# Modulation products moved from GpSimd and ScalarE to VectorE, and spread over three feed-forward stretches

## The chip, the cores and the metric

The kernel runs on one core of one Trainium2 chip. The core has TensorE (PE in the profile's rows, PEld for its weight loads), VectorE (DVE), ScalarE (ACT), GpSimd (POOL) and SyncE (SP, which here only issues DMAs). Each engine takes its own instructions in order, and they wait for one another through semaphores. The metric is the device time of one execution in microseconds (us).

## The reference, cut to what matters

Two blocks run one after the other, each with two layers, on 512 tokens of width 1024. A layer of the first block is a mixer, an attention over a memory of 256 tokens, and a gated feed-forward network (FFN). A layer of the second block is a local attention and an FFN, for the 512 tokens and, in its first layer alone, for a context of 256 tokens too. The second block scales and shifts its normalised inputs, and gates its outputs, with a modulation that depends on two vectors only, `c` for the tokens and `c_ctx` for the context:

```python
for i in range(DEPTH):                    # the second block, DEPTH = 2
    last = i == DEPTH - 1
    mod = silu(c) @ w_mod[i] + b_mod[i]          # 1024 -> 6 * 1024
    mod_c = silu(c_ctx) @ w_mod[i] + b_mod[i]
    sh1, sc1, gt1, sh2, sc2, gt2 = jnp.split(mod[:, None, :], 6, axis=-1)
    sh1c, sc1c, gt1c, sh2c, sc2c, gt2c = jnp.split(mod_c, 6, axis=-1)
    h = modulate(rmsnorm(x, g_attn[i]), sh1, sc1)
    hc = modulate(rmsnorm(ctx, g_attn[i]), sh1c, sc1c)
    ...                                   # attention; x = x + gt1 * (o @ w_out)
    h = modulate(rmsnorm(x, g_ffn[i]), sh2, sc2)
    x = x + gt2 * conv_ffn(h, ...)
    if not last:
        ...                               # the same for ctx with gt1c, sh2c, sc2c, gt2c
```

So `w_mod` (two layers of 24 MB) meets only two vectors, and in the last layer the context needs nothing beyond `sh1c` and `sc1c`, the first 16 of 48 groups of 128 outputs.

## The kernel before

All activations lie with their features on the 128 partitions, in tiles of 128 x 512 (tokens) or 128 x 256 (context). A linear layer is exact to nearly full precision by splitting: each operand is the sum of a rounded high part and a low part, and `lin` issues three matmuls for each 128 x 128 weight tile (high x high, high x low, low x high). A weight of 128 x 1024 (eight of those tiles) comes in through `wload` (L318 to L332): SyncE loads it into a buffer `wr` (two of them), ScalarE writes its high part `wh` (L314), VectorE its low part `wl` (L331, `wr - wh`); there are three buffers of `wh` and three of `wl`. TensorE needs both parts of a weight, and gives them back when it is through with it. A new activation is split in the same way (`split`: L314 on ScalarE, then L317 on VectorE).

`ffn1` is the first block's FFN, 22 units of 2816 / 128 features. For each unit `up` makes two products of 24 matmuls, scales each with the norm's factor out of PSUM (L1178), and runs a three-tap convolution over the tokens (one tap on ScalarE, L1181, two on VectorE, L1183), a Silu, the gate product (L1186) and the split. The units come in parts of 6, 6, 5 and 5 (`F1_PARTS`); each part's down-projection (8 tiles of features, `down`, added to `x` at L1199) waits in a queue and is issued tile by tile among the units of the next part.

`ffn2` is the second block's FFN. In the first layer it runs two streams, tokens and context, with the same weights: `up` copies PSUM out on ScalarE, `conv` does all three taps on VectorE (L2025, L2027), `gate` the gate and split. It has parts of 8, 7 and 7 units (`FF_PARTS`), and each part's down-projection follows its units at once (`down`, L2084). Matmul results go to PSUM banks with the tags L, S, PT and O; the up-products of this stretch use L (two banks; S for some of the first eight).

The modulation doesn't use TensorE. `mod_steps` (L1246) is a generator. A step loads one 128 x 512 tile of `w_mod` (256 KB, 96 of them for a layer), multiplies it with the two vectors, which lie broadcast over the partitions, and sums each product along its row into one column of `mparts`. Of eight products VectorE does two, in one instruction with a row sum (L1282); GpSimd does six as a plain product (L1284), which ScalarE copies with a row sum three products later (L1262). `mem_attn` of first-block layer `i` starts the steps of second-block layer `i`, and `ffn1` goes on with them after each unit: two steps for a unit of the first part, five for the others (`F1_MOD`). So each of the two first-block FFNs carries a whole layer of the modulation, 192 products.

[...]

Of the kernel before, what the change touches and what calls it, by code (L numbers as in the profile page):

```python
# [14 lines left out]
AF = mybir.ActivationFunctionType  # L15
# [22 lines left out]
MSTEP = (0,1,4,1,2)  # L38
MDN = (0,0,2)
MH = 48  # L40
MLAG = 3
# [21 lines left out]
MPF = 4  # L63
MODV = (0,4)
# [23 lines left out]
F1_MOD = (2, 5, 5, 5)  # L88
# [170 lines left out]
class Builder:  # L259
# [804 lines left out]
    def mem_attn(self, i, f, mh, K, fn):  # L1064
# [17 lines left out]
        self.steps = self.mod_steps(i, 0, 96)  # L1082
# [66 lines left out]

    def step(self, n, r):  # L1150
# [6 lines left out]
    def ffn1(self, i, f, fn):  # L1157
# [5 lines left out]

        def bank():
            self.bank += 1
            return self.p(FTAGS[self.bank % len(FTAGS)])

# [78 lines left out]
    def mod_steps(self, i, n0, n1):  # L1246
        nc = self.nc
        cv = []
        for v in range(2):
            for e in range(2):  # L1250
# [4 lines left out]
            yield  # L1255
        part = self.mparts
        late = []

        def add(k):
            while len(late) > k:  # L1260
                o, t = late.pop(0)
                nc.scalar.activation(t, t, AF.Copy, accum_out=o)  # L1262

        ws = {}

        def load(n):
            if n < n1:
                ws[n] = self.t("A", [P, 512])
                nc.sync.dma_start(out=ws[n], in_=self.a["w_mod"][i, n // 2, n % 2])

        for n in range(n0, n0 + MPF):
            load(n)
        for n in range(n0, n1):
            load(n + MPF)
            m, e = divmod(n, 2)
            w = ws.pop(n)
            for v in range(2):
                t = self.t("A", [P, 512])
                self.modn += 1
                o = part[:, v, e, m:m + 1]  # L1280
# [6 lines left out]
            yield  # L1287
        add(0)
        if n1 == 96:
            for v in range(2):  # L1290
                mo = self.mod[i][:, :, v]
                nc.vector.tensor_add(out=mo, in0=part[:, v, 0], in1=part[:, v, 1])
# [931 lines left out]
```

## Time and profile before

| | before |
|---|---|
| median of 3 runs (lowest to highest), us | 3841.25 (3839.11 to 3844.32) |
| the profiled execution: its time, us | 3832.78 |
| its span, first to last instruction, us | 3831.0 |
| busy: TensorE matmuls / weight loads | 3675.2 (96%) / 3062.5 (80%) |
| busy: VectorE / ScalarE / GpSimd | 2669.1 (70%) / 1842.9 (48%) / 1001.0 (26%) |
| mean granted TensorE clock | 0.988 of full speed |

The span holds these stretches: the first block's mixers and memory attentions with its FFNs at about 694 to 1090 us and 1740 to 2142 us, the second block's first attention, its first FFN (both streams) at about 2617 to 3172 us, the second attention, and the last FFN (tokens alone) from 3464 us to the end. A share of busy time is a mean over stretches with different limits, and TensorE's busy time is longer where its clock is lower.

### The profile page before, as it was taken

The numbers are of one execution on the slowest core, as the hardware profiler recorded it, in microseconds if no ns is written. First come the engines' busy times: TensorE is split into PE (matmuls) and PEld (weight loads), VectorE is DVE, ScalarE is ACT, GpSimd is POOL, SyncE is SP. The second block draws the span as 40 slices with busy tenths as digits, with TensorE's granted clock in tenths as the row PEclk, the third lists the DMA queues.
The fourth block names the chain that finished last, engine by engine and source line by source line (L and its number), as shares of the span: only waits on it lengthen the run. The fifth ranks groups of instructions, "written<-read, shape, count | busy, mean of one in ns | idle before, by whom it ended". The sixth has DMA issues, their size and how long they took to land. (4 is left out here: it accounts for less than half of the span.)

```text
span 3831.0 us, 55553 instructions
## 1 busy us (share of the span) xinstructions
PE 3675.2 (96%) x21300; PEld 3062.5 (80%) x21300; DVE 2669.1 (70%) x4599; ACT 1842.9 (48%) x3532; POOL 1001.0 (26%) x688
## 2 busy tenths in 40 slices
PE   8999999999899999999999899899999999999999
PEld 6777788777778777887777899778888888888887
DVE  7768756889977687668998753777545547657555
ACT  5645634455555456344555454774222225554232
POOL 1223243467621121234666212321000012100000
PEclk9999999999999999999999999999999999999999
DMA  3222143344422211333444332322212212012232
GB/s 112 67 72 67 51 127 100 111 154 157 146 91 72 72 57 56 126 105 102 165 155 150 123 104 92 108 73 72 66 61 61 66 56 74 15 40 93 94 95 93
DMA packets 128714, 354.39 MB, mean 93 GB/s; under 512 B 14144, under 2 KB 26816, under 8 KB 128448
## 3 DMA queue, kind: packets, MB, share of 16 engines
q1 hardware_dynamic: 127440, 349.62, 28.6%
q8 instruction: 168, 2.75, 0.3%
q10 hardware_dynamic: 1008, 1.21, 0.1%
q14 instruction: 98, 0.80, 0.1%
HBM read 346.58 MB, written 4.19 MB: 92 GB/s over the span
## 5 line engine op out<-in xcount | busy, mean ns | idle before, releaser
L304 PE MATMUL L<-A,wh 128*128 128x512 f32 (+1 forms) x6408 | 1861.5, 375 | 19.5 <-ACT wh L314 8.8
L304 PEld LDWEIGHTS L<-A,wh 128*128 128x128 f32 x6408 | 1148.0, 189 | 241.7 <-ACT wh L314 13.1
L304 PE MATMUL L<-A,wl 128*128 128x512 f32 (+1 forms) x3204 | 1194.9, 373 | 20.4 <-DVE wl L331 19.8
L314 ACT ACTIVATE wh<-wr 128x1024 fp32r<-128x1024 f32 (+4 forms) x562 | 561.9, 1001 | 787.7 <-PE L L304 429.8
L331 DVE TENSOR_TENSOR wl<-wr,wh 128x1024 fp32r<-128x1024 f32 (+4 forms) x503 | 658.7, 1311 | 327.2 <-ACT wh L314 319.1
L304 PEld LDWEIGHTS L<-A,wl 128*128 128x128 f32 x3204 | 604.7, 189 | 137.5 <-DVE wl L331 26.3
L1284 POOL TENSOR_TENSOR A<-A,A 128x512 f32<-128x512 f32 x288 | 482.3, 1706 | 280.6 <-DMA A<-in_w_mod 169.2
L304 PE MATMUL S<-A,wh 128*128 128x512 f32 (+1 forms) x944 | 301.0, 400 | 25.6 <-ACT wh L314 14.7
L331 POOL TENSOR_TENSOR wl<-wr,wh 128x1024 fp32r<-128x1024 f32 (+1 forms) x59 | 139.4, 2363 | 547.4 <-ACT wh L314 473.4
L304 PE MATMUL L<-wh,A 128*128 128x256 f32 x1440 | 272.7, 285 | 2.3 <-ACT A L1309 2.0
L304 PE MATMUL PT<-A,wh 128*128 128x512 f32 (+1 forms) x904 | 262.1, 375 | 0.0
L304 PEld LDWEIGHTS S<-A,wh 128*128 128x128 f32 x944 | 180.9, 195 | 70.8 <-ACT wh L314 16.5
L1183 DVE SCALAR_TENSOR_TENSOR A<-A,vec,A 128x512 f32<-128x512 f32 x176 | 215.2, 1223 | 30.6 <-ACT A L1181 26.4
L304 PEld LDWEIGHTS L<-wh,A 128*128 128x128 f32 x1440 | 226.0, 189 | 8.1 <-issue 4.2
L304 PE MATMUL O<-A,A 128*64 128x128 f32 (+3 forms) x2528 | 228.1, 288 | 4.2 <-DVE A L648 3.6
L433 POOL TENSOR_TENSOR acc<-acc,A 128x512 f32<-128x512 f32 (+1 forms) x44 | 53.8, 1222 | 672.1 <-ACT A L427 670.2
L304 PE MATMUL L<-wl,A 128*128 128x256 f32 x720 | 204.6, 284 | 4.6 <-DVE wl L331 4.6
L304 PEld LDWEIGHTS O<-A,A 128*64 128x64 f32 (+1 forms) x2528 | 168.5, 143 | 48.6 <-issue 24.0
L304 PE MATMUL S<-A,wl 128*128 128x512 f32 (+1 forms) x472 | 189.8, 402 | 17.8 <-DVE wl L331 17.6
L1262 ACT ACTIVATE A<-A 128x512 f32<-128x512 f32 x288 | 177.3, 618 | 38.5 <-POOL A L1284 38.3
L304 PEld LDWEIGHTS PT<-A,wh 128*128 128x128 f32 x904 | 166.7, 191 | 32.7
L314 ACT ACTIVATE A<-A 128x512 fp32r<-128x512 f32 (+2 forms) x202 | 115.3, 571 | 147.4 <-DVE A L1186 78.1
(323 smaller groups left out, 5249.7 us busy)
## 6 DMA issues: line engine op xcount, KB each, us to landing
wr<-in_w_up SPq DMA_DIRECT2D x176, 512.0 KB
A<-in_w_mod SPq DMA_DIRECT2D x192, 256.0 KB
wr<-in_w_qkv SPq DMA_DIRECT2D x62, 512.0 KB
wr<-in_w_in SPq DMA_DIRECT2D x60, 512.0 KB
wr<-in_w_down SPq DMA_DIRECT2D x32, 448.0 KB
wr<-in_w_down SPq DMA_DIRECT2D x32, 384.0 KB
wr<-in_w_down SPq DMA_DIRECT2D x32, 320.0 KB
wr<-in_w_os SPq DMA_DIRECT2D x16, 512.0 KB
```

Source lines behind the costliest of these rows:

```text
L304: self.last_mm = self.nc.tensor.matmul(out, lhsT=l, rhs=r, start=start, stop=stop, skip_group_check=True)
L314: self.nc.scalar.activation(h, src, AF.Copy)
L331: eng.tensor_sub(out=l[:, :cols], in0=r[:, :cols], in1=h[:, :cols].bitcast(F32))
L433: self.mark_p = (add or nc.gpsimd).tensor_add(out=acc.t, in0=acc.t, in1=dst)
L1183: ve.scalar_tensor_tensor(out=ac, in0=u[:, tap:tap + S], scalar=cw(tap), in1=ac, op0=ALU.mult, op1=ALU.add)
L1262: nc.scalar.activation(t, t, AF.Copy, accum_out=o)
L1284: nc.gpsimd.tensor_mul(out=t, in0=w, in1=cv[2 * v + e])
```

## The change

Every product of the modulation that is still made is made on VectorE, in one instruction with its row sum (now L1274). GpSimd's products and ScalarE's row sums are gone. The steps are laid out anew:

- Second-block layer 0: `mod_steps(0, 24 * i, 24 * i + 24)`. The memory attention and FFN of first-block layer 0 do output groups 0 to 23, those of layer 1 groups 24 to 47: 48 steps and 96 products each.
- Second-block layer 1: `mod_steps(1, 0, 48)` inside `ffn2` of the second block's first layer, its steps set off after the up-products (0.7 a product, none in a part's last unit) and the down-products (1.2 each). Context products are made for 16 of the 48 groups: 96 steps, 128 products.
- A pass of `mod_steps` goes first through the half `e = 0` of all its groups and then through `e = 1`. It loads two vectors for each half, and two tiles of `w_mod` ahead (`MPF`, four before).
- That FFN has parts of 6, 6, 5 and 5 units, and all its results rotate through PSUM tags L, S and PT.

```diff
-MSTEP = (0,1,4,1,2)
+MSTEP = (0,0.5)
...
-MPF = 4
-MODV = (0,4)
+MPF = 2
...
-F1_MOD = (2, 5, 5, 5)
+F1_MOD = (1, 2.5, 2.5, 2.5)
+F2_PARTS = ((0, 6), (6, 6), (12, 5), (17, 5))
+F2_MOD = (0.7, 1.2)
...
-        self.steps = self.mod_steps(i, 0, 96)
+        self.steps = self.mod_steps(0, 24 * i, 24 * i + 24)
...
-    def mod_steps(self, i, n0, n1):
+    def mod_steps(self, i, m0, m1):
...
+        nv = lambda m: 2 if i < DEPTH - 1 or m < 16 else 1
+        for e in range(2):
+            cv = []
+            for v in range(2):
                 c = self.t("A", [P, 512])
                 nc.sync.dma_start(out=c, in_=self.a["cvec"][v, e])
                 nc.scalar.activation(c, c, AF.Silu)
                 cv.append(c)
...
-                if self.modn % 8 in MODV:
-                    nc.vector.scalar_tensor_tensor(out=t, in0=w, scalar=1.0, in1=cv[2 * v + e], op0=ALU.mult, op1=ALU.mult, accum_out=o)
-                else:
-                    nc.gpsimd.tensor_mul(out=t, in0=w, in1=cv[2 * v + e])
-                    late.append((o, t))
-            add(MLAG)
-            yield
...
+            for m in range(m0, m0 + MPF):
+                load(m)
+            for m in range(m0, m1):
+                load(m + MPF)
+                w = ws.pop(m)
+                for v in range(nv(m)):
+                    t = self.t("A", [P, 512])
+                    nc.vector.scalar_tensor_tensor(out=t, in0=w, scalar=1.0, in1=cv[v], op0=ALU.mult, op1=ALU.mult,
+                                                   accum_out=part[:, v, e, m:m + 1])
+                yield
...
+        bank = self.next_bank if both else lambda: self.p("L")
+        fparts = F2_PARTS if both else FF_PARTS
+        if both:
+            self.bank = 0
+            self.steps = self.mod_steps(1, 0, 48)
...
+                        if both and j < j0 + nj - 1:
+                            self.step(4 * j + 2 * e + 1 - s, F2_MOD[0])
...
                 down(m, s)
+                if both:
+                    self.step(n, F2_MOD[1] if pi < 3 else 100)
```

The order of TensorE's matmuls in the first block's FFNs stays as it was. Three places show what moves.

GpSimd, in the first block's first FFN, before: nothing but the modulation's products stands in its queue (`A` tiles: the product, the tile of `w_mod`, a vector). Here are six of them.

```order
L1284 TENSOR_TENSOR A_7124<-A_6958,A_5899 128x512
L1284 TENSOR_TENSOR A_7126<-A_6958,A_5944 128x512
L1284 TENSOR_TENSOR A_7132<-A_6966,A_5902 128x512
L1284 TENSOR_TENSOR A_7139<-A_6973,A_5899 128x512
L1284 TENSOR_TENSOR A_7141<-A_6973,A_5944 128x512
L1284 TENSOR_TENSOR A_7147<-A_7115,A_5902 128x512
```

In the changed kernel this FFN has no row on GpSimd at all: all 288 rows of L1284 are gone, and the last sum of squares of the memory attention is followed by the next mixer's first rows.

VectorE, in the third part of the same FFN, before: the low parts of weights (`wl`), the scaling out of PSUM, the taps, the gate, a down tile added to `x`, the split of the unit, and then its share of the products.

```order
L331 TENSOR_TENSOR wl_8106<-wr_8104,wh_8105 128x768
L1177 MEMSET A_8027 128x2
L1183 SCALAR_TENSOR_TENSOR A_7992<-A_7989,vec,A_7992 128x512 x2
L1178 TENSOR_TENSOR A_8027<-PT_7996,rs_6308 128x512
L331 TENSOR_TENSOR wl_8132<-wr_8130,wh_8131 128x1024
L1183 SCALAR_TENSOR_TENSOR A_8030<-A_8027,vec,A_8030 128x512 x2
L1186 TENSOR_TENSOR A_8030<-A_7992,A_8030 128x512
L1199 TENSOR_TENSOR x<-x,L_8077 128x512
L331 TENSOR_TENSOR wl_8170<-wr_8168,wh_8169 128x1024
L317 TENSOR_TENSOR A_8037<-A_8030,A_8036 128x512
L1282 SCALAR_TENSOR_TENSOR A_8044,mparts<-A_7876,A_5947 128x512
L1282 SCALAR_TENSOR_TENSOR A_8059,mparts<-A_7891,A_5947 128x512
```

The changed kernel at such a unit:

```order
L331 TENSOR_TENSOR wl_7578<-wr_7576,wh_7577 128x1024
L1184 SCALAR_TENSOR_TENSOR A_7477<-A_7474,vec,A_7477 128x512 x2
L1179 TENSOR_TENSOR A_7512<-S_7481,rs_6280 128x512
L331 TENSOR_TENSOR wl_7616<-wr_7614,wh_7615 128x1024
L1184 SCALAR_TENSOR_TENSOR A_7515<-A_7512,vec,A_7515 128x512 x2
L1187 TENSOR_TENSOR A_7515<-A_7477,A_7515 128x512
L1200 TENSOR_TENSOR x<-x,PT_7549 128x512
L331 TENSOR_TENSOR wl_7672<-wr_7670,wh_7671 128x768
L317 TENSOR_TENSOR A_7522<-A_7515,A_7521 128x512
L1274 SCALAR_TENSOR_TENSOR A_7525,mparts<-A_7405,A_5938 128x512
L1274 SCALAR_TENSOR_TENSOR A_7527,mparts<-A_7405,A_5941 128x512
L1274 SCALAR_TENSOR_TENSOR A_7529,mparts<-A_7411,A_5938 128x512
```

The work of the unit is the same; four to six products stand behind its split where two or three stood.

VectorE, in the second block's first FFN, at the start of a part's down-projection, before (a part of eight units): after the unit's last split come, for each tile of features, two results added out of PSUM and the next weight's low part.

```order
L317 TENSOR_TENSOR A_25895<-A_25811,A_25894 128x512
L2020 MEMSET A_26393 128x1
L2021 MEMSET A_26393 128x1
L2084 SCALAR_TENSOR_TENSOR A_18673<-L_25898,mod_108,A_18673 128x256
L2084 SCALAR_TENSOR_TENSOR x<-L_25899,mod_108,x 128x512
L331 TENSOR_TENSOR wl_26075<-wr_26073,wh_26074 128x1024
L2084 SCALAR_TENSOR_TENSOR A_18673<-L_25956,mod_108,A_18673 128x256
L2084 SCALAR_TENSOR_TENSOR x<-L_25988,mod_108,x 128x512
L331 TENSOR_TENSOR wl_26133<-wr_26131,wh_26132 128x1024
```

The changed kernel at the end of its first part of six units: the last rows ahead of the low part of the fourth down weight (`S`, `PT`: PSUM results; L1274: products; L2082: results added). Between the part's last split and the first row here stand five more products and two more results.

```order
L1274 SCALAR_TENSOR_TENSOR A_24868,mparts<-A_24825,A_24138 128x512
L1274 SCALAR_TENSOR_TENSOR A_24892,mparts<-A_24832,A_24135 128x512
L1274 SCALAR_TENSOR_TENSOR A_24894,mparts<-A_24832,A_24138 128x512
L2082 SCALAR_TENSOR_TENSOR x<-S_24870,mod_108,x 128x512
L1274 SCALAR_TENSOR_TENSOR A_24924,mparts<-A_24864,A_24135 128x512
L1274 SCALAR_TENSOR_TENSOR A_24926,mparts<-A_24864,A_24138 128x512
L1274 SCALAR_TENSOR_TENSOR A_24930,mparts<-A_24890,A_24135 128x512
L2082 SCALAR_TENSOR_TENSOR A_17802<-PT_24896,mod_108,A_17802 128x256
L1274 SCALAR_TENSOR_TENSOR A_24932,mparts<-A_24890,A_24138 128x512
L1274 SCALAR_TENSOR_TENSOR A_24956,mparts<-A_24922,A_24135 128x512
L1274 SCALAR_TENSOR_TENSOR A_24958,mparts<-A_24922,A_24138 128x512
L331 TENSOR_TENSOR wl_24963<-wr_24961,wh_24962 128x768
```

So 14 products and four results, where two results stood before each weight, come between the last split and that weight's low part. For the two parts that follow, five products stand in that place.

## Rows read from the trace of the kernel before

**Rows 1.** Four FFN stretches: length, busy PE PEld DVE ACT POOL, PEclk, DMA.

```profile
694.00:1090.00 396.00, 375.12 (x1580) 298.75 (x1579) 354.32 (x435) 217.18 (x443) 242.48 (x144) 0.98 0.45 144
1740.00:2142.00 402.00, 376.11 (x1573) 300.19 (x1572) 351.22 (x455) 219.86 (x457) 226.39 (x135) 0.96 0.44 142
2617.00:3172.00 555.00, 552.22 (x3139) 480.86 (x3137) 308.47 (x668) 161.93 (x267) 15.01 (x12) 1.00 0.20 62
3464.00:3831.00 367.00, 362.44 (x1604) 294.42 (x1602) 218.06 (x368) 118.71 (x162) 0.00 (x0) 1.00 0.30 95
```

**Rows 2.** The chain that ended last, its final piece: start, length, what.

```profile
3464.96 361.49 PE L L304 x1597
```

**Rows 3.** TensorE's waits in 694:1090, 1740:2142: us in total, times, longest.

```profile
PE S L304 <- DVE wl L331: 8.1, 4, 3.6
...
PE S L304 <- DVE wl L331: 8.7, 5, 3.6
...
PE O L304 <- DVE acc L433: 3.1, 1, 3.1
```

**Rows 4.** Six stretches of halved clock in those windows: first, and sum.

```profile
769.40:776.20 6.80, 4.88 (x12) 0.50 0.29 89
...
sum 37.40, PE 28.58; mean PE 4.76
```

**Rows 5.** VectorE's groups by form in 694:1090: busy, mean ns, idle before.

```profile
L1183 DVE SCALAR_TENSOR_TENSOR A<-A,vec,A 128x512 f32<-128x512 f32 x88 | 105.9, 1204 | 15.0 <-ACT A L1181 13.4 <-issue 0.2
L331 DVE TENSOR_TENSOR wl<-wr,wh 128x1024 fp32r<-128x1024 f32 x43 | 66.8, 1553 | 10.5 <-ACT wh L314 10.5
L1282 DVE SCALAR_TENSOR_TENSOR A<-A,A 128x512 f32<-128x512 f32 x45 | 57.2, 1295 | 0.0
L1178 DVE TENSOR_TENSOR A<-S,rs 128x512 f32<-128x512 f32 x18 | 12.3, 681 | 1.9 <-ACT rs L404 1.9
```

**Rows 6.** The same view in 3475:3831, where GpSimd does nothing.

```profile
L2027 DVE SCALAR_TENSOR_TENSOR A<-A,vec,A 128x512 f32<-128x512 f32 x88 | 66.0, 751 | 2.6
L331 DVE TENSOR_TENSOR wl<-wr,wh 128x1024 fp32r<-128x1024 f32 x48 | 58.7, 1225 | 47.2 <-ACT wh L314 46.3
```

**Rows 7.** The page, costliest groups: busy us, mean ns, idle before: GpSimd's products.

```profile
L1284 POOL TENSOR_TENSOR A<-A,A 128x512 f32<-128x512 f32 x288 | 482.3, 1706 | 280.6 <-DMA A<-in_w_mod 169.2
```

**Rows 8.** Timeline around 685 us, GpSimd and VectorE: start, length.

```profile
678.65 10.60 POOL L1284 TENSOR_TENSOR A<-A,A 128x512 f32<-128x512 f32 x7
...
685.47 1.32 DVE L369 TENSOR_SCALAR rt<-rt 128x4 int32<-128x4 int32 x1
...
689.20 0.15 DVE L370 TENSOR_SCALAR rt<-rt 128x4 int32<-128x4 int32 x1
```

**Rows 9.** Timeline near 1001 us: products of VectorE, one after another.

```profile
1001.08 0.69 DVE L1282 SCALAR_TENSOR_TENSOR A<-A,A 128x512 f32<-128x512 f32 x1
1001.69 0.08 DVE L1282 DVE_READ_ACCUMULATOR A<-A,A 128x1 f32 x1
1001.69 0.69 DVE L1282 SCALAR_TENSOR_TENSOR A<-A,A 128x512 f32<-128x512 f32 x1
```

**Rows 10.** TensorE's waits in 672:694 and 1718:1740, the norm's factor.

```profile
PE O L304 <- DVE rt L379: 3.3, 1, 3.3
...
PE O L304 <- DVE rt L379: 2.1, 1, 2.1
```

**Rows 11.** Second block's first FFN, 2617:3115: VectorE's groups by form.

```profile
L2084 DVE SCALAR_TENSOR_TENSOR x<-L,mod,x 128x512 f32<-128x512 f32 x16 | 12.0, 751 | 67.0 <-PE L L304 67.0
L2084 DVE SCALAR_TENSOR_TENSOR A<-L,mod,A 128x256 f32<-128x256 f32 x16 | 7.7, 483 | 9.7 <-PE L L304 9.7
```

**Rows 12.** Timeline, same FFN: a weight's high part, released by TensorE, and low part.

```profile
2762.22 1.06 ACT L314 ACTIVATE wh<-wr 128x1024 fp32r<-128x1024 f32 x1 [7.54 <-PE L L304]
2763.31 1.23 DVE L331 TENSOR_TENSOR wl<-wr,wh 128x1024 fp32r<-128x1024 f32 x1 [0.15 <-ACT wh L314]
```

**Rows 13.** All waits: GpSimd's products for their tiles of `w_mod`.

```profile
POOL A L1284 <- DMA A<-in_w_mod: 169.2, 29, 14.4
```

More of the change, by code (lines that the diff above doesn't have):

```diff
@@ L1147, in mem_attn, with next_bank @@
             self.step(m, MSTEP[1])
+    def next_bank(self):
+        self.bank += 1
+        return self.p(FTAGS[self.bank % len(FTAGS)])
     def step(self, n, r):
@@ L1243, in mod_prep @@
         self.G = [[self.c([P, KD, 2], name=f"G{i}{j}") for j in range(2)] for i in range(DEPTH)]
-    def mod_steps(self, i, n0, n1):
+    def mod_steps(self, i, m0, m1):
         nc = self.nc
-        cv = []
-        for v in range(2):
-            for e in range(2):
+        part = self.mparts
+        nv = lambda m: 2 if i < DEPTH - 1 or m < 16 else 1
+        for e in range(2):
+            cv = []
+            for v in range(2):
                 c = self.t("A", [P, 512])
@@ L1254, in mod_steps @@
                 cv.append(c)
-            yield
[L1256 to L1276, printed above, removed]
-            for v in range(2):
-                t = self.t("A", [P, 512])
-                self.modn += 1
-                o = part[:, v, e, m:m + 1]
-                if self.modn % 8 in MODV:
-                    nc.vector.scalar_tensor_tensor(out=t, in0=w, scalar=1.0, in1=cv[2 * v + e], op0=ALU.mult, op1=ALU.mult, accum_out=o)
-                else:
-                    nc.gpsimd.tensor_mul(out=t, in0=w, in1=cv[2 * v + e])
-                    late.append((o, t))
-            add(MLAG)
-            yield
@@ L1288, in mod_steps, with load @@
[L1288 to L1292, printed above, removed]
-                nc.vector.tensor_add(out=mo, in0=mo, in1=self.v(f"b_mod{i}"))
+            ws = {}
+            def load(m):
+                if m < m1:
+                    ws[m] = self.t("A", [P, 512])
+                    nc.sync.dma_start(out=ws[m], in_=self.a["w_mod"][i, m, e])
+            for m in range(m0, m0 + MPF):
+                load(m)
@@ new lines, in mod_steps @@
+            for m in range(m0, m1):
[6 more added lines that the diff above has]
+                yield
+        if m1 == 48:
+            for v in range(2):
+                n = 48 if nv(47) > v else 16
+                mo = self.mod[i][:, :n, v]
+                nc.vector.tensor_add(out=mo, in0=part[:, v, 0, :n], in1=part[:, v, 1, :n])
+                nc.vector.tensor_add(out=mo, in0=mo, in1=self.v(f"b_mod{i}")[:, :n])
@@ L1294, in mod_steps @@
             for j, gn in ((0, "g_attn"), (1, "g_ffn")):
-                for s in range(2):
-                    nc.vector.scalar_tensor_tensor(out=self.G[i][j][:, :, s], in0=self.mod[i][:, 24 * j + 8:24 * j + 16, s], scalar=1.0,
+                for v in range(2 if j == 0 else nv(47)):
+                    nc.vector.scalar_tensor_tensor(out=self.G[i][j][:, :, v], in0=self.mod[i][:, 24 * j + 8:24 * j + 16, v], scalar=1.0,
                                                    in1=self.v(f"{gn}{i}"), op0=ALU.add, op1=ALU.mult)
@@ L2006, in ffn2, with up @@
         w, ab = {}, {}
-        def up(j, e, s, tag="L"):
+        both = rc is not None
+        bank = self.next_bank if both else lambda: self.p("L")
[3 more added lines that the diff above has]
+            self.steps = self.mod_steps(1, 0, 48)
+        def up(j, e, s):
             rhs, n = streams[s]
@@ L2034, in gate @@
             return self.split(A)
-        for pi, (j0, nj) in enumerate(FF_PARTS):
+        for pi, (j0, nj) in enumerate(fparts):
             act = {s: [] for s in streams}
-            last = pi == len(FF_PARTS) - 1
+            last = pi == len(fparts) - 1
             first = 0
@@ L2042, in ffn2 @@
                 for j, e, s in ((0, 0, 1), (0, 1, 1), (1, 0, 1), (0, 0, 0), (0, 1, 0), (1, 1, 1), (1, 0, 0), (1, 1, 0)):
-                    up(j, e, s, "S" if s else "L")
+                    up(j, e, s)
                     if e == 1:
@@ L2080, in down @@
                 else:
-                    ps = self.p("L")
+                    ps = bank()
                     self.lin(ps[:, :n], weights(m), act[s])
@@ L2175, in build @@
         self.setup()
-        self.modn = 0
         self.mod_prep()
```

9 lines of the change are left out of this document (3 added, 6 removed).

## The prediction

> **What bounds the kernel now.** I read first the page's busy times: TensorE is busy for 96% of the span, so an edit can only win where TensorE idles, waits, or runs on a lowered clock. Then a table of the four FFN stretches [rows 1]. An FFN on the 512 tokens is 44 x 24 + 8 x 22 x 3 = 1584 matmuls of 128 x 512 in either block. The last one of the kernel runs without a pause: the chain's last piece is 361.5 us for 1597 matmuls, 0.226 us each [rows 2]. The two first-block FFNs, the same number of matmuls, take 396 and 402 us in their windows, and TensorE is idle there for 20.9 and 25.9 us [rows 1]. The waits in these windows say on whom: the longest are on `wl` of L331, the low part of a weight, which VectorE writes [rows 3]. Besides, the granted clock falls to half (0.50, which is 1.2 GHz of 2.4) six times in them, each time just after TensorE had stood still for such a wait; together 37.4 us [rows 4].
>
> So VectorE is late. It is busy for 354.3 and 351.2 us in these stretches [rows 1], which is 98% of the 361.5 us that the matmuls need: any unevenness stops TensorE. Why it needs that long is seen by comparing forms. A tap of the convolution (L1183) takes 1204 ns here, the same instruction (L2027) takes 751 ns in the last FFN; a low part of 1024 columns takes 1553 ns against 1225 [rows 5, 6]. The difference between the stretches is GpSimd, busy for 242.5 us in the one and for none of the other [rows 1], with products of 1706 ns [rows 7]. An instruction with one input in PSUM, L1178, keeps its 681 ns beside GpSimd [rows 5]. The clearest place is near 685 us: while GpSimd runs seven products in a row, a VectorE instruction on four elements takes 1.32 us, and its like takes 0.15 us once they are over [rows 8].
>
> The Trainium skill has this as a rule (SBUF — State Buffer, Who interferes with whom): "A DVE instruction with two SBUF inputs contends with a GpSimd instruction that reads SBUF", and whichever comes second is blocked. The trace agrees, with 1204 against 751 ns, and 681 ns for the form with one SBUF input.
>
> **The change, part by part.** I make the sum against the profiled execution: 3832.8 us, 3831.0 of it span. The median of the runs is 3841.25, 8.5 us above; I carry the difference over.
>
> *A, waits in the first-block FFNs.* GpSimd falls silent there. VectorE loses, per FFN: 88 taps x (1.204 - 0.751) = 39.9 us, 43 low parts x (1.553 - 1.225) = 14.1 us, 45 products of 1.295 = 58.3 us [rows 5, 6]. It gains 88 products (96 less the eight made in the memory attention). What one costs undisturbed is seen where two follow each other: 0.69 us long, and 0.61 us from start to start, the reading of the sum included [rows 9]. 88 x 0.69 = 60.7 us. New need: 354.3 - 39.9 - 14.1 - 58.3 + 60.7 = 302.7 us, 84% of 361.5 instead of 98%. ScalarE, which loses 144 row sums, was not what TensorE waited for. The idle time to win is 20.9 + 25.9 - 3.1 us (a wait for the context's sum of squares at the end of the second FFN, which stays [rows 3]) = 43.7 us.
>
> *B, the clock.* 37.4 us at half speed cost half of it [rows 4]: 18.7 us. The dips follow the waits of A and go with them.
>
> Not all of A and B will go. A weight still passes through load, ScalarE and VectorE with two `wr` buffers, and VectorE's work is uneven. I take 90% of 62.4 us: 56.2; bounds 50% and 100%.
>
> *C, the start of each FFN.* The norm's factor is a chain of tiny VectorE instructions; where GpSimd runs beside it one takes 1.32 us and not 0.15 [rows 8], and TensorE waits 3.3 and 2.1 us for the end of the chain [rows 10]. Three instructions that get 1.2 us shorter are enough to take that away. 5.4 us; bounds 2 and 8, as the low part and split just ahead of it get shorter too.
>
> *D, the second block's first FFN* pays. There TensorE hardly idles (552.2 of 555 us) and VectorE is busy for 308.5 [rows 1]. It gets 128 products x 0.69 = 88.3 us, and with a fourth part eight more results of each kind, 8 x (0.751 + 0.483) = 9.9 us [rows 11]: 407 us, 73%. What covers this is the lead of the weights: with three buffers, ScalarE starts on one when TensorE still has two to go, in the down-projections 2 x 18 x (0.226 + 0.113) = 12.2 us, less 2.3 us from there to the low part's end [rows 12]: 9.9 us. If the cover is gone, every us counts. The tightest place is in the listing of the order: 14 products and four results before the fourth down weight of the first part. VectorE: 14 x 0.61 + 2 x (0.751 + 0.483) + 0.92 (1.225 us scaled to 768 columns) = 11.9 us; with 0.77 us per product, reading apart, 14.2. TensorE, from the last split on: 1.0 + 2 x 6.1 = 13.2 us. So between 1.3 us early and 1.0 late. In the later parts five products stand there, and nothing is late. The fourth part also adds an end where TensorE waits for a last split; the matmuls that the order has ready there (6.7, 6.7, 6.1 and 6.3 us by 0.226 each, against 7.7, 6.7 and 6.3) cost at most 1 us.
>
> The moved loads are the part I can't price from a row. Two products use a tile of 256 KB in 1.2 us, 215 GB/s, on top of 64 GB/s of down weights; the first-block FFNs ran at 144 GB/s at a DMA share of 0.45 [rows 1], which would be 320 at full share by my estimate. If 144 were the limit, seven tiles and two weights (2.6 MB) would need 18.2 us instead of 13.2: 5 us late, and a clock dip of 6.8 us would cost 3.4 more. Behind a product that waits for its tile stand the low parts, on VectorE; ahead of a weight on SyncE stand tiles that wait for a free `A` buffer. By the order a tile's buffer is free some ten VectorE instructions (about 7 us) before its product. Lower end 0, upper end 10; I take 4 in all, nearer to the lower end, as VectorE had no idle time ahead of its own products in the first-block FFN, their tiles were there [rows 5].
>
> Sum: 56.2 + 5.4 - 4 = 57.6 us off: 3831.0 becomes 3773.4 us of span, and the median 3841.25 becomes **3784 us**.
>
> **The rivals.** *Half stays* (0.14): in the first-block FFNs the weights' way through two `wr` buffers, not VectorE's speed, decides half of the waits. 31.2 + 5.4 - 4 = 32.6: 3809 us. For it: all of TensorE's waits are at weights. Against it: the last FFN has the same path and no wait [rows 2].
>
> *The second block pays* (0.13): tiles come late at the down-projections of three parts, each time 5 + 1 + 3.4 = 9.4 us. 61.6 - 28.2 = 33.4: 3808 us. For it: three VectorE-dense stretches. Against it: only one has two products a tile at such a pace throughout.
>
> *VectorE stops for its tiles* (0.04, slower): GpSimd waited 29 times, 169.2 us in all, for `w_mod` [rows 13]. It had nothing else to do; on VectorE everything queues behind such a wait. If all of it showed on TensorE, 169.2 - 57.6 = 111.6 more: 3953 us. The kernel gets slower from 57.6 us of such waits, a third of them, on. Against it: GpSimd waited because it ran ahead of the loads, while VectorE's own products, in order behind other work, had no idle time before them [rows 5].
>
> *The change doesn't do what it says* (0.02): the 1.2 us are these instructions' own price under the load of that stretch. Then VectorE, at 98%, gets 43 products of 1.295 us more, 55.7 us per FFN, and sets the pace: about 3841 + 111 + 4 = 3956 us. Against it stand the short forms in the same stretch [rows 8, 9]. The Trainium skill's advice for a full VectorE points this way too (Perfetto Trace Analysis, Optimizing Scalar/DVE Operations): "offloading some work to Scalar (or even GPSIMD) may make sense", so taking the offload back would cost; it adds in the same place that the two share a read port.
>
> **How the numbers follow.** The forecast has 0.65; by its bounds (A and B from 75% to all, D from 0 to 10) it runs from 3773 to 3799 us. 0.02 is left for more than that, when the other dips at the FFNs' ends go too, down to some 3765. The range takes in the two rivals near 3809 with their spread: 3765 to 3815. What a measurement of this kernel can tell is about 0.2%, 8 us. All cases but the two slow ones lie below 3833: faster 0.93; same 0.03; slower 0.04, the two slow rivals less a part in which they are mild.
>
> **What would show it.** In the changed profile: L1184 near 750 ns and low parts near 1225 in the first-block FFNs; products at 0.69; VectorE busy about 300 us in each, GpSimd nearly none; those FFNs some 30 us shorter each, with clock dips gone but at their ends; TensorE's wait for the norm's factor gone; the second block's first FFN about 4 us longer, with VectorE at some 400 us. I am wrong if products show waits for `w_mod`, if taps stay at 1200 ns, or if TensorE goes on waiting for `wl` in the first-block FFNs.

## The result, and the profile after

| | before | after |
|---|---|---|
| median of the runs (lowest to highest), us | 3840.18 (3837.0 to 3844.32) | 3749.23 (3747.13 to 3749.81) |
| the profiled execution: time / span, us | 3832.78 / 3831.0 | 3749.81 / 3748.0 |
| busy: TensorE matmuls, us | 3675.2 | 3649.7 |
| busy: VectorE / ScalarE / GpSimd, us | 2669.1 / 1842.9 / 1001.0 | 2621.8 / 1675.8 / 524.9 |

The ratio is 0.9762, with an interval from 0.9745 to 0.9778: 91 us faster, where 57.6 were forecast. The direction and the mechanism were right, the size was not, and the time lies below the range (3765 to 3815 us).

Where the time went is read from whole stretches, cut at the last output result of a memory attention (the last row of L1145, added to `x`), the last down-result of an FFN and, in the second block, the first convolution result of an FFN. The first two rows are the first-block FFNs, the third is the second block's first FFN with the attention behind it. Columns are as in [rows 1]. The kernel before:

```profile
673.30:1084.10 410.80, 382.22 (x1601) 304.53 (x1600) 363.86 (x459) 220.58 (x450) 254.24 (x154) 0.97 0.44 141
1720.10:2142.10 422.00, 390.31 (x1624) 311.32 (x1623) 363.26 (x472) 224.83 (x466) 242.27 (x147) 0.96 0.43 139
2623.90:3474.60 850.70, 837.46 (x5674) 735.84 (x5673) 509.27 (x1040) 321.15 (x601) 60.11 (x58) 1.00 0.18 56
```

The changed kernel, the same three stretches:

```profile
672.90:1042.80 369.90, 369.70 (x1607) 300.04 (x1606) 291.69 (x538) 137.59 (x176) 23.56 (x15) 1.00 0.40 125
1681.20:2054.60 373.40, 372.32 (x1635) 302.21 (x1633) 292.94 (x559) 144.90 (x193) 12.37 (x8) 1.00 0.40 126
2541.10:3392.50 851.40, 836.00 (x5658) 734.71 (x5657) 594.85 (x1327) 325.63 (x613) 59.80 (x58) 1.00 0.27 87
```

The two FFNs are 40.9 and 48.6 us shorter, 89.5 in all, and TensorE is busy for practically all of them at a full clock (1.00, which is 2.4 GHz). The second block, which got 128 products, is 0.7 us longer. What is left, 5.8 us, was lost in the stretches between: 89.5 - 0.7 - 5.8 = 83.0 us, the difference of the spans. The cuts don't fall on quite the same matmul in both kernels (the counts behind TensorE's busy time): the third stretch holds 16 fewer after. Taken over the same matmuls it is some 3 us longer, and the two FFNs some 92 us shorter.

VectorE's groups by form in the first of these FFNs, after:

```profile
L1184 DVE SCALAR_TENSOR_TENSOR A<-A,vec,A 128x512 f32<-128x512 f32 x88 | 65.9, 749 | 7.0 <-ACT A L1182 5.4
L331 DVE TENSOR_TENSOR wl<-wr,wh 128x1024 fp32r<-128x1024 f32 x45 | 57.4, 1275 | 11.2 <-ACT wh L314 11.0
L1274 DVE SCALAR_TENSOR_TENSOR A<-A,A 128x512 f32<-128x512 f32 x90 | 57.3, 687 | 0.2 <-DMA A<-in_w_mod 0.2
...
L331 DVE TENSOR_TENSOR wl<-wr,wh 128x768 fp32r<-128x768 f32 x16 | 15.3, 957 | 1.5 <-ACT wh L314 1.5
...
L1179 DVE TENSOR_TENSOR A<-S,rs 128x512 f32<-128x512 f32 x18 | 12.4, 691 | 20.8 <-PE S L304 18.7 <-ACT rs L404 1.9
```

Beside [rows 5]: a tap fell from 1204 to 749 ns, a low part from 1553 to 1275, a product from 1295 to 687; the form with an input in PSUM stayed nearly as it was (681 and 691). VectorE waits for ScalarE in front of its low parts about as long as before (11.2 us, 10.5 in [rows 5]); what is new is that it waits for TensorE's results, 20.8 us in the last line, where it was 1.9. So VectorE now has time to spare. The low parts of 768 columns, which the prediction did not price, got shorter too. Before, in the first FFN:

```profile
L331 DVE TENSOR_TENSOR wl<-wr,wh 128x768 fp32r<-128x768 f32 x16 | 24.0, 1501 | 5.4 <-ACT wh L314 5.4
```

TensorE's waits in these two FFNs, where [rows 3] and [rows 10] had 8.1, 8.7 and 3.3 us, are one each. The first FFN:

```profile
PE O L304 <- DVE rt L379: 0.2, 1, 0.2
```

The second FFN:

```profile
PE PT L304 <- DVE wl L331: 0.9, 1, 0.9
```

In the second block's first FFN the products are hidden though VectorE does stop for tiles, 6.5 us in all:

```profile
L1274 DVE SCALAR_TENSOR_TENSOR A<-A,A 128x512 f32<-128x512 f32 x128 | 84.6, 686 | 6.5 <-DMA A<-in_w_mod 6.5
```

### The profile page after: what moved, and what is told of

It is laid out like the page before. It is cut to its first block, busy times and chain, and to the rows that moved or that the text cites. A ratio compares the mean times of both kernels' runs of the same rounds, so it can differ in the third digit from the quotient of the medians.

```text
span 3748.0 us, 54845 instructions
## 1 busy us (share of the span) xinstructions
PE 3649.7 (97%) x21300; PEld 3053.8 (81%) x21300; DVE 2621.8 (70%) x5070; ACT 1675.8 (45%) x2968; POOL 524.9 (14%) x400
## 5 line engine op out<-in xcount | busy, mean ns | idle before, releaser
L304 PE MATMUL L<-A,wh 128*128 128x512 f32 (+1 forms) x5060 | 1519.5, 382 | 14.1 <-ACT wh L314 4.5
L304 PEld LDWEIGHTS L<-A,wh 128*128 128x128 f32 x5060 | 914.2, 189 | 201.0 <-issue 12.7
L304 PE MATMUL L<-A,wl 128*128 128x512 f32 (+1 forms) x2530 | 960.0, 380 | 5.5 <-DVE wl L331 4.9
L304 PE MATMUL S<-A,wh 128*128 128x512 f32 (+1 forms) x1592 | 461.2, 373 | 11.6 <-ACT wh L314 8.9
L304 PE MATMUL PT<-A,wh 128*128 128x512 f32 (+1 forms) x1604 | 431.5, 356 | 0.0
L304 PE MATMUL PT<-A,wl 128*128 128x512 f32 (+1 forms) x802 | 285.4, 356 | 0.9 <-DVE wl L331 0.9
L1274 DVE SCALAR_TENSOR_TENSOR A<-A,A 128x512 f32<-128x512 f32 x320 | 212.8, 705 | 7.6 <-DMA A<-in_w_mod 6.7
L433 POOL TENSOR_TENSOR acc<-acc,sq 128x512 f32<-128x512 f32 (+1 forms) x80 | 128.8, 1610 | 420.3 <-ACT sq L427 411.3
L2023 DVE SCALAR_TENSOR_TENSOR A<-A,vec,A 128x512 f32<-128x512 f32 (+1 forms) x264 | 173.6, 661 | 5.0
L304 PEld LDWEIGHTS S<-A,wl 128*128 128x128 f32 x796 | 150.1, 189 | 27.8 <-DVE wl L331 0.8
```

Of the source, the lines that this page charges most:

```text
L304: self.last_mm = self.nc.tensor.matmul(out, lhsT=l, rhs=r, start=start, stop=stop, skip_group_check=True)
L433: self.mark_p = (add or nc.gpsimd).tensor_add(out=acc.t, in0=acc.t, in1=dst)
L2023: ve.scalar_tensor_tensor(out=ac, in0=u[:, tap:tap + n], scalar=cw(tap), in1=ac, op0=ALU.mult, op1=ALU.add)
```

## The experiments

Theory 1: GpSimd's reads lengthen VectorE's instructions, VectorE then has more to do than an FFN's matmuls take, weights are late, TensorE stands still and its clock falls. Theory 2: the new layout (half of the products in an FFN) gives the gain. Open besides: what the starts of the FFNs are worth, whether ScalarE's relief counts, and what the second block paid. Windows below are whole FFNs, cut as above; their columns are those of [rows 1].

### Products on VectorE, nothing else changed

On the kernel before:

```diff
-MODV = (0,4)
+MODV = (0,1,2,3,4,5,6,7)
```

> The kernel before with all products on VectorE and nothing else changed: each first-block FFN still carries a whole layer, 96 steps and 192 products, and the second block's first FFN is as it was. Theory 1 (GpSimd's reads slow VectorE, and that made the FFNs long): the taps go back to about 750 ns and the low parts to 1225 though VectorE makes 184 products in each FFN; VectorE's work there is the 285 us of the changed kernel + 96 x 0.69 = 352 us, under the 362 us of the matmuls, and the two FFN stretches take 371 to 385 us instead of 412 and 423: 3755 to 3790 us. Theory 2 (the gain comes from the new layout, since each FFN has half of the products): taps stay short or not, but with twice the products VectorE is late again, the FFN stretches stay at about 410 us and the time at 3820 us or more.

Measured: 3759.79 us (3752.4 to 3763.95), ratio 0.979 (0.9765 to 0.9816). The two FFNs:

```profile
676.70:1049.10 372.40, 369.81 (x1600) 298.51 (x1599) 343.26 (x732) 136.91 (x173) 24.05 (x15) 1.00 0.47 154
1687.10:2065.40 378.30, 372.95 (x1624) 302.19 (x1624) 344.36 (x744) 141.66 (x189) 12.83 (x8) 1.00 0.47 153
```

Its products and taps in the first:

```profile
L1282 DVE SCALAR_TENSOR_TENSOR A<-A,A 128x512 f32<-128x512 f32 x182 | 114.5, 692 | 0.0
L1183 DVE SCALAR_TENSOR_TENSOR A<-A,vec,A 128x512 f32<-128x512 f32 x88 | 65.1, 747 | 3.3 <-ACT A L1181 2.6
```

This one edit gives 81 of the 91 us. VectorE makes 182 products instead of 46 and is busy for 343 us, 21 fewer than before. Theory 2 falls as the main cause; the rest of the change adds the last 10 us, by the medians of two comparisons, and 7 of them lie in these two FFNs.

### The new layout with GpSimd's products

On the changed kernel, for the second block's layer 0 alone (`add` lets ScalarE sum the products of `late`, as before):

```diff
+MLAG = 3
+MODV = (0,4)
...
-                    nc.vector.scalar_tensor_tensor(out=t, in0=w, scalar=1.0, in1=cv[v], op0=ALU.mult, op1=ALU.mult,
-                                                   accum_out=part[:, v, e, m:m + 1])
+                    o = part[:, v, e, m:m + 1]
+                    self.modn += 1
+                    if i or self.modn % 8 in MODV:
+                        nc.vector.scalar_tensor_tensor(out=t, in0=w, scalar=1.0, in1=cv[v], op0=ALU.mult, op1=ALU.mult, accum_out=o)
+                    else:
+                        nc.gpsimd.tensor_mul(out=t, in0=w, in1=cv[v])
+                        late.append((o, t))
+                add(MLAG)
...
```

> The changed kernel, but in the first-block FFNs six of eight products are made on GpSimd again, with ScalarE's row sums; layout, parts and banks stay new. Theory 1 in the form that VectorE's sum decides: 66 products fewer on VectorE in an FFN save 45 us, and 66 on GpSimd cost it about 0.6 us each, 40 us: VectorE's work stays near 280 us, so the FFN stretches stay at 371 to 376 us, 3750 to 3765 us in all. Theory 1 in the form that each single delay shows (a low part that is late by a product's contention stops TensorE at once, whatever VectorE's sum): half of the 89 us won in the two stretches is lost again, about 3795 us. Theory 2 (the layout gives the gain): no difference, 3750 us.

Measured: 3761.84 us (3759.85 to 3764.26), ratio 0.9798 (0.9775 to 0.9822).

```profile
672.60:1048.50 375.90, 371.38 (x1603) 301.12 (x1602) 284.19 (x404) 178.57 (x309) 128.81 (x82) 0.99 0.39 125
1685.80:2065.90 380.10, 375.49 (x1632) 303.44 (x1631) 286.14 (x426) 184.07 (x326) 115.91 (x75) 1.00 0.39 125
```

This is what VectorE's sum foretold (up to 3765), and not the half of the 89 us that each single delay would cost. 67 products left VectorE in the first FFN, at 0.61 us from start to start [rows 9] that is 41 us; its busy time fell by 7.5. So a product on GpSimd took about 0.5 us of VectorE's time. What the kernel loses, it loses at the start, and there a single delay does show at once, though VectorE has room: TensorE waits for the norm's factor, and its clock is at half behind that for 6.8 us. The wait in the first FFN (3.2 us in the second):

```profile
PE O L306 <- DVE rt L381: 4.3, 1, 4.3
```

### The same without products beside the norm's factor

On that kernel, in the memory attention and the FFN:

```diff
-            self.step(m, MSTEP[1])
...
-F1_MOD = (1, 2.5, 2.5, 2.5)
+F1_MOD = (1.7, 2.5, 2.5, 2.5)
```

> The changed layout with six of eight products on GpSimd in the first-block FFNs, as once before, but none in the memory attention: its four steps go into the FFN's first part. The kernel with GpSimd's products in the new layout lost 12.6 us against the changed one, and the trace shows waits at the FFNs' starts alone (4.3 and 3.2 us for the norm's factor, a clock dip of 6.8 and 3.4 us behind them) and none for a weight in the FFNs. If this is term C, products beside the norm's factor, the waits and dips go and the FFNs fall from 376 and 380 us to 371 to 374: 3748 to 3754 us. If the waits move elsewhere, as they did when the kernel before lost its products in the attention: 3758 to 3763 us.

Measured: 3750.57 us (3748.7 to 3752.13), ratio 0.9775 (0.9757 to 0.9794): 1.3 us from the changed kernel by the medians, 5 by the ratios, whose intervals overlap.

```profile
673.60:1043.20 369.60, 369.56 (x1607) 300.12 (x1606) 284.62 (x407) 184.68 (x324) 133.84 (x87) 1.00 0.40 131
1681.70:2056.80 375.10, 373.63 (x1635) 302.20 (x1633) 283.58 (x427) 190.73 (x340) 123.09 (x80) 1.00 0.40 131
```

The waits for the norm's factor and the dips behind them are gone, with five products of GpSimd and one of VectorE taken out of the memory attention ahead of the first FFN. ScalarE has its row sums here, 185 us of work against 138, and it shows nowhere: with room on VectorE, ScalarE's relief gave nothing.

### No products in the attention, in the kernel before

The same on the kernel before:

```diff
-            self.step(m, MSTEP[1])
...
-F1_MOD = (2, 5, 5, 5)
+F1_MOD = (2.7, 5, 5, 5)
```

> The kernel before, but the memory attention makes no products: its eight steps go into the first part of the FFN (2.7 steps a unit instead of 2). What is asked is how much of the loss lies at the FFNs' starts, outside the part that the prediction summed: before, TensorE waits there 8.1 and 5.8 us (for the norm's factor and for A of L437 and L438), and its clock is at half for 6.8 and 10.2 us. If products beside the last tiles of the attention cause these, they go: 13.9 + 8.5 = 22 us at most, less up to 5 us for the eight steps that the FFNs get on top: 3818 to 3828 us. If the starts wait for something else, nothing goes and the added steps cost: 3841 to 3846 us.

Measured: 3831.59 us (3824.24 to 3839.33), ratio 0.9984 (0.9974 to 0.9995): 6 us, by the interval 2 to 10.

```profile
666.60:1077.60 411.00, 386.21 (x1606) 306.55 (x1606) 370.35 (x464) 227.80 (x467) 266.16 (x159) 0.97 0.45 148
1718.60:2134.90 416.30, 388.01 (x1632) 307.69 (x1631) 368.56 (x476) 231.90 (x483) 255.03 (x152) 0.97 0.44 148
```

Here neither expectation held. The start waits are gone from the trace, as in the kernel above. The second FFN got 5.7 us shorter, but the first takes as long as before: its waits for low parts grew instead. Before, they were the 8.1 us of [rows 3] and this line, 15.6 us together:

```profile
PE L L304 <- DVE wl L331: 7.5, 5, 3.0
```

Without products in the attention they are 21.3 us, on three lines:

```profile
PE S L304 <- DVE wl L331: 8.9, 6, 3.6
PE L L304 <- DVE wl L331: 8.3, 6, 3.1
PE PT L304 <- DVE wl L331: 4.1, 3, 3.2
```

So with VectorE this full, a stall taken away at the start came back elsewhere in one of the two FFNs; part of that can be the eight products that this FFN got on top. With room on VectorE the like edit of the kernel above was worth 9 us by the ratios and 11 by the medians, about what its waits and dips had cost, with six products moved into the first FFN and not eight.

### Unused work on GpSimd: products, one product, zeros, copies

On the changed kernel, behind the two products of each step of the second block's layer 0 (in the first-block FFNs, and in the few steps of each memory attention; `range(1)` in the second kernel):

```diff
+                if i == 0:
+                    for _ in range(3):
+                        nc.gpsimd.tensor_mul(out=t, in0=w, in1=cv[0])
```

in the third `nc.gpsimd.memset(t, 0.0)`, and in the fourth `nc.gpsimd.tensor_copy(out=t, in_=w)`, three times each.

> The changed kernel, with three plain products on GpSimd added to each step of the first-block FFNs; they read the same tile and vector, write over VectorE's unused result, and nobody uses them. VectorE, ScalarE and the loads do what they did. Theory 1: about 138 such products in an FFN of some 1.7 us each; VectorE's taps and low parts get longer as in the kernel before (about 1.2 and 1.55 us), its work goes from 285 to some 365 us, TensorE waits for low parts and its clock dips again; the FFN stretches get 30 us longer each or more: 3800 us or more. Theory 2 (layout) and the rival that ScalarE's relief gave the gain: no difference, within 5 us of 3749 us.

> The changed kernel with one unused GpSimd product a step instead of three, about 45 in each first-block FFN. With three, VectorE's work there went over 361 us and the kernel lost 125 us. If VectorE's sum decides (285 + 45 x 0.6 = 312 us, under 361 us): a loss of 0 to 12 us, 3749 to 3761 us, most of it where products fall together with a late weight. If the loss goes with the number of contended us: a third of 125 us, about 3790 us.

> As the kernel with the unused products, but GpSimd only writes: three times a step it fills VectorE's unused result with zeros. Theory 1 as the trace of before has it (it is GpSimd's reading that gets in VectorE's way): taps stay at about 750 ns, and the time within 5 us of 3749 us. The rival that any GpSimd access to the memory, or its mere work, slows VectorE: the taps get longer by as much per us of GpSimd's busy time as beside the products.

> The changed kernel with three unused copies a step on GpSimd instead of products: one input from memory, one result. Filling with zeros (69 us of GpSimd in an FFN) left the taps at 749 ns; products with two inputs (221 us) made them 1224 ns. If any reading by GpSimd gets in VectorE's way, the taps get longer in proportion to the copies' busy time, +2.1 ns for each us of it, and the kernel loses time as soon as VectorE's sum is over 350 us. If only two-input instructions of GpSimd do, the taps stay at 749 ns and the time at 3749 us, as with the zeros.

Measured: three products 3873.54 us (3872.11 to 3878.25), ratio 1.0088 (1.0059 to 1.0116), slower than the kernel before; one product 3752.77, 0.9779 (0.9764 to 0.9793); zeros 3748.25, 0.9763 (0.974 to 0.9787); copies 3751.98, 0.9765 (0.9746 to 0.9785). The first FFN with three products:

```profile
676.20:1101.90 425.70, 384.79 (x1603) 305.01 (x1602) 389.81 (x539) 136.68 (x176) 250.99 (x155) 0.97 0.35 110
```

with one product:

```profile
673.70:1044.50 370.80, 369.92 (x1607) 300.04 (x1606) 319.86 (x540) 137.71 (x176) 91.19 (x60) 1.00 0.39 126
```

with zeros:

```profile
670.20:1041.00 370.80, 369.87 (x1608) 300.17 (x1607) 292.30 (x540) 137.88 (x176) 93.95 (x150) 1.00 0.39 124
```

with copies:

```profile
672.70:1043.90 371.20, 369.81 (x1606) 300.10 (x1606) 316.51 (x540) 137.76 (x176) 144.15 (x151) 1.00 0.39 125
```

and, in that FFN, the taps and VectorE's products beside three products, the taps and GpSimd's own row beside zeros, and the same two beside copies:

```profile
L1184 DVE SCALAR_TENSOR_TENSOR A<-A,vec,A 128x512 f32<-128x512 f32 x88 | 107.7, 1224 | 6.5 <-ACT A L1182 5.3
L1274 DVE SCALAR_TENSOR_TENSOR A<-A,A 128x512 f32<-128x512 f32 x90 | 94.2, 1095 | 0.4 <-DMA A<-in_w_mod 0.4
```

```profile
L1184 DVE SCALAR_TENSOR_TENSOR A<-A,vec,A 128x512 f32<-128x512 f32 x88 | 65.8, 749 | 7.0 <-ACT A L1182 5.6
...
L1278 POOL MEMSET A<- 128x512 f32 x135 | 70.1, 526 | 265.8 <-DVE A L1274 241.9 <-PE S L304 10.0 <-DVE A L1178 8.4
```

```profile
L1184 DVE SCALAR_TENSOR_TENSOR A<-A,vec,A 128x512 f32<-128x512 f32 x88 | 74.4, 846 | 6.8 <-ACT A L1182 5.4
...
L1278 POOL COPY A<-A 128x512 f32<-128x512 f32 x135 | 119.4, 892 | 216.9 <-DVE A L1274 113.1 <-issue 89.0 <-PE L L304 9.1
```

Nobody used GpSimd's results, VectorE's instructions were the same, and yet VectorE's busy time rose from 291.7 to 389.8 us: 98 us for 138 products, 0.71 us each. It did not wait for its tiles there (0.4 us), so the unused products did not harm by holding buffers back. One product a step cost 28 us for 45, 0.63 each, and the FFN only 0.9 us, since 320 us still fit. Zeros (526 ns each, 70 us in all) cost VectorE nothing; copies (892 ns, 119 us in all) cost it 0.18 us each and the taps 97 ns. On a tap that is 0.8 ns for each us that GpSimd copied, against 2.1 for products: the proportion that was expected of "any reading" fell, and so did "only two-input instructions". The taps alone are no full measure: beside one product a step they stayed at 748 ns, and the delay fell on VectorE's products (915 ns) and low parts (1384). By VectorE's whole busy time, a us of GpSimd's copies cost 0.21 us and a us of its products 0.42 to 0.43.

The Trainium skill (SBUF — State Buffer, Who interferes with whom) says that VectorE with two SBUF inputs contends with a GpSimd instruction that reads SBUF, and not with one that only writes it. The runs agree, with 1224, 846 and 749 ns.

### The same load on VectorE itself

As with three products, but `nc.vector.tensor_mul(out=t, in0=w, in1=cv[0])`.

> The changed kernel with three unused products a step on VectorE itself in the first-block FFNs, and GpSimd silent. 135 products of 0.69 us in an FFN put 93 us on VectorE's 292: 385 us, about what three unused products on GpSimd made of it (390 us, FFNs of 426 and 442 us). If it is VectorE's sum that decides, however it comes about, the FFNs take 405 to 435 us and the kernel 3820 to 3870 us. If a product beside VectorE does harm beyond VectorE's sum (its delays fall on the low parts that TensorE needs next), the FFNs here take little more than VectorE's 385 us: 3780 us.

Measured: 3806.09 us (3800.61 to 3808.65), ratio 0.9905 (0.9879 to 0.9931).

```profile
674.00:1068.30 394.30, 378.39 (x1592) 304.21 (x1591) 366.95 (x675) 140.06 (x175) 24.46 (x16) 0.97 0.36 119
1707.80:2106.70 398.90, 382.48 (x1622) 307.08 (x1621) 368.08 (x695) 144.99 (x191) 14.49 (x9) 0.97 0.36 119
```

Between the two expectations. With GpSimd nearly silent and VectorE at 367 us, the FFNs are 24 and 26 us longer than in the changed kernel; those of before, with VectorE at 364 and 363, were 41 and 49 us longer. So VectorE's sum explains the larger part, and some 17 and 23 us come on top. That before also had twice the tiles to load and ScalarE's sums was not taken apart from GpSimd's bad moments; each cost next to nothing where VectorE had room (the first and the third experiment), but this share at full load stays open.

Put side by side, VectorE's busy time in the first FFN and that FFN's length:

| kernel | VectorE, us | FFN, us |
|---|---|---|
| new layout, GpSimd's products | 284.2 | 375.9 |
| the same, none in the attention | 284.6 | 369.6 |
| changed kernel | 291.7 | 369.9 |
| zeros on GpSimd | 292.3 | 370.8 |
| copies on GpSimd | 316.5 | 371.2 |
| one unused product on GpSimd | 319.9 | 370.8 |
| old layout, all on VectorE | 343.3 | 372.4 |
| before | 363.9 | 410.8 |
| three unused products on VectorE | 367.0 | 394.3 |
| before, no products in the attention | 370.4 | 411.0 |
| three unused products on GpSimd | 389.8 | 425.7 |

In the changed kernel TensorE is busy for the whole of this FFN, 369.9 us. Up to 343 us of VectorE's time, 93% of that, at most 2.5 us are lost, but for the first row, whose 6 us are the wait for the norm's factor and the dip behind it; from 364 us on, at least 24.

### What the second block paid

This kernel leaves out the second layer's modulation:

```diff
-            self.steps = self.mod_steps(1, 0, 48)
+            self.steps = iter(())
+            for z in [self.mod[1]] + self.G[1]:
+                ve.memset(z, 0.0)
```

> The changed kernel without the second layer's modulation: no loads, products or sums for it, and zeros in place of its shifts, scales and gates. Parts and banks of the second block's first FFN stay new. Prediction's term D (the second block pays about 4 us for the 128 products): 3745 us. If the products are fully hidden there: no difference in the FFN, 3749 us; and if the 4 us that the second attention got longer come from the end of these steps, these 4 us go: 3745 us, but in the attention's stretch and not in the FFN's.

With the old parts, and tag L for all results:

```diff
-        bank = self.next_bank if both else lambda: self.p("L")
-        fparts = F2_PARTS if both else FF_PARTS
+        bank = lambda: self.p("L")
+        fparts = FF_PARTS
...
-                    self.step(n, F2_MOD[1] if pi < 3 else 100)
+                    self.step(n, F2_MOD[1] if pi < 2 else 100)
```

> The changed kernel, but the second block's first FFN has three parts of 8, 7 and 7 units again and takes its up- and down-products' results from the two banks of tag L; the 128 products stay in it. If the new banks and parts gave the 3.7 us by which that FFN got shorter, it goes back to 547 us or more: 3753 to 3765 us, with TensorE waiting for banks or for low parts behind products. If the 3.7 us came from elsewhere (nothing ahead of it on GpSimd, other starts): no difference, 3749 us.

And the same with tag S for the first context results, so that parts and banks are those of before:

```diff
-                    up(j, e, s)
+                    up(j, e, s, "S" if s else "L")
```

> As the kernel with three parts and the banks of tag L in the second block's first FFN, but its first context results go to tag S again, as in the kernel before; without that, TensorE stood 8.0 us at this FFN's start. If the new parts and banks are needed to hide the 128 products, the FFN and the attention behind it still take some 3 us or more longer than the 851.5 us of the changed kernel together: 3753 us or more. If the start was all, 3749 us, within 2 us.

Measured: 3748.3 us (3747.11 to 3749.63), ratio 0.9768 (0.9754 to 0.9782); 3757.03 (3752.65 to 3761.1), 0.9791 (0.9775 to 0.9806); 3749.21 (3746.81 to 3752.32), 0.9759 (0.9738 to 0.978). This FFN and the attention behind it, without the second layer's products:

```profile
2539.50:3391.10 851.60, 836.11 (x5659) 734.91 (x5658) 520.04 (x1065) 323.78 (x609) 58.99 (x58) 1.00 0.17 56
```

With the old parts and tag S:

```profile
2541.70:3393.40 851.70, 838.67 (x5674) 736.84 (x5673) 585.04 (x1303) 322.72 (x605) 60.03 (x58) 1.00 0.26 87
```

851.6 us without the 128 products, 851.4 with them in the new parts and banks; 851.7 with them in the old ones, 850.7 before: the products cost about nothing, and neither the parts nor the banks were needed to hide them. The new parts and banks did cost something, which the cuts hide, as the first two of these windows hold 15 or 16 matmuls fewer than the other two (5659 and 5658 against 5674). In the second attention TensorE waits for the norm's factor three times, in the changed kernel and without the products,

```profile
PE O L304 <- DVE rt L379: 5.9, 3, 2.5
```

```profile
PE O L304 <- DVE rt L379: 6.2, 3, 2.8
```

and once, as in the kernel before, with the old parts and tag S:

```profile
PE O L304 <- DVE rt L379: 2.5, 1, 2.5
```

The FFN alone had looked 3.7 us shorter after; the attention behind it was longer by more, so the border had moved. In the FFN, what mattered is where the first results go: with tag L for all of them TensorE stood still at the start.

```profile
PE L L304 <- ACT A L2018: 8.0, 1, 8.0
```

## Why the prediction was too small

**The step that failed** is the sum of A, B and C: it took 90% of the waits and dips inside 694:1090 and 1740:2142 and left the borders of these windows at zero, but for the norm's factor. All of it went, and the borders too: the starts and ends gave 28 us, where C had 5.4 and at most 8. In the kernel before, four more dips lie at the borders or were left out as belonging to the FFN's end:

```profile
680.60:687.40 6.80, 5.90 (x18) 5.03 (x19) 5.68 (x7) 1.78 (x3) 6.80 (x6) 0.50 0.25 78
1728.50:1735.30 6.80, 6.80 (x21) 5.65 (x22) 5.69 (x8) 1.06 (x1) 6.80 (x6) 0.50 0.14 57
1738.80:1742.20 3.40, 3.40 (x12) 2.82 (x12) 0.81 (x3) 1.41 (x2) 0.00 (x0) 0.51 0.35 130
2110.80:2117.60 6.80, 5.94 (x18) 5.11 (x19) 3.15 (x10) 2.72 (x5) 0.00 (x0) 0.50 0.00 0
sum 23.80, PE 22.04 PEld 18.60 DVE 15.33 ACT 6.97 POOL 13.60; mean PE 5.51 PEld 4.65 DVE 3.83 ACT 1.74 POOL 3.40
```

and beside the waits for the norm's factor, TensorE had waited at the FFNs' starts for the first split inputs. At the first:

```profile
PE S L304 <- ACT A L437: 2.5, 1, 2.5
PE S L304 <- DVE A L438: 2.3, 1, 2.3
```

At the second they were 1.4 and 2.3 us.

- **A and B**, 43.7 + 18.7 us: all of it, where 90% were taken (6.2 us short). The discount stood for the weights' way through two `wr` buffers; with VectorE at 292 us it was late once, for 0.9 us. VectorE was relieved of more than the 52 us that A has: of 72, as low parts of 768 and 640 columns and splits got shorter as well. The FFN got 90 products and not 88, as six and not eight fell to the attention.
- **C**, 5.4 us: gone, one wait of 0.2 us is left. The waits for split inputs (8.5 us) went with it, and half of the four dips (11.9), three of them behind the starts' waits and one behind the wait of 3.1 us for the sum of squares. That wait, which was to stay, went too, against a new one of 0.9 us. Together 22.6 us short. A, B and C so add up to 43.7 + 18.7 + 5.4 + 22.6 = 90.4 us, against 89.5 measured.
- **D**, -4 us: 0.7 was paid by the cuts, some 3 over the same matmuls, and that is not the products' doing. VectorE was busy for 595 us in the stretch and not 509, its tiles were late for 6.5 us in all, and the lead of the weights covered it, as D's lower end had it. What was paid are the waits for the norm's factor in the attention behind, 5.9 us and not 2.5, with the new parts and banks; D had no such term. That its size comes near is luck.
- **What the prediction did not have**: 5.8 us lost between the FFNs, 4.7 of them in the second block's first attention (481.8 before, 486.5 after). No kernel here edits that attention's code, and it took from about 481 to 488 us in them, 487 in the one with the old layout and all products on VectorE, so this was not laid to the change.
- **The median**: the profiled execution of before lies 7.4 us under the median of this comparison; it was carried over. The changed kernel's lies 0.6 us above its own. 83.0 + 7.4 + 0.6 = 91.0. So 25.4 us of the 33.4 that were missed lie in the span, and 8.0 in carrying that difference over.

The mechanism held at the points that the prediction named: taps at 749 ns, products at 687, GpSimd nearly silent in the FFNs, dips gone. Low parts of 1024 columns stayed at 1275 ns, 50 above the 1225 named. Of the rivals, "half stays" was wrong, as all went, and "the second block pays" too, as no tile came late for TensorE there. "VectorE stops for its tiles" was right that it would wait for some, and wrong that it mattered. "The change doesn't do what it says" fell with the first experiment. The case that all ends and dips go had been given 0.02.

## What to carry to other kernels

Compare a helper engine's busy time with the length of the stretch that it must feed, stretch by stretch: here 93% cost 2.5 us and 98 to 99% cost 24 to 41. Once it is well below, expect all waits on it and the clock dips behind them to go, those at the ends of the stretch too, but for short chains that something else delays, as GpSimd's products did the norm's factor at 284 us. Cut windows at the borders of the stretch, not inside, and see that they hold the same matmuls. Handing GpSimd products with two SBUF inputs was little or no relief for VectorE beside its own two-input instructions: each took 0.5 to 0.71 us of VectorE, which makes one itself in 0.61.

## What was not expected of the hardware

- Stalls are not additive. No products beside the norm's factor: with VectorE at 98% this took away 13.9 us of waits and 17 us at half clock at the starts, and gave 6 us (2 to 10); with room on VectorE it took away 7.5 us of waits and 10.2 us at half clock, and gave 9 to 11.
- Zeros on GpSimd left VectorE's times as they were, and a copy cost it a quarter to a third of what a product does (0.18 against 0.5 to 0.71 us), half for the same GpSimd time.
- A profiled execution can lie 7 or 8 us off its kernel's median, and that difference need not carry over: the four runs of the kernel before spread over 7.3 us, those of the changed one over 2.7. What sets the spread is not shown; the old layout with all products on VectorE, which hardly stalls, spread over 11.6.
